# Applying the SSD's group norm to the tiles in the SSD stage instead of to the output projection's partial sums

## The chip, the cores and the metric

One core of a Trainium2 chip runs the whole layer. The metric is the device time of one execution in microseconds (us). An execution keeps five engines busy: TensorE (PE in the profile, with its weight loads as PEld), VectorE (DVE), ScalarE (ACT), GpSimd (POOL) and SyncE (SP), which issues nearly all DMAs here. Each engine works through its own instructions in a fixed order and waits where an operand is not ready.

## The reference, cut to what matters

The layer mixes two branches of 1024 columns each, a Mamba-2 SSD and a stick-breaking attention, projects their concatenation and goes on to a SwiGLU FFN. The part that the change concerns is the end of the SSD branch: two groups of 512 columns, each with its own RMS norm after the gate.

```python
y = y.reshape(bsz, seq, D_SSD) * silu(z)
yg = y.reshape(bsz, seq, SSD_GROUPS, D_SSD // SSD_GROUPS)
yg = yg * rsqrt(mean(yg * yg, axis=-1, keepdims=True) + EPS)
y_ssd = yg.reshape(bsz, seq, D_SSD) * norm_w
...
mix = concatenate([y_ssd, y_sb], axis=-1) @ w_out
```

The norm's factor is one number per token and group. It can be applied to the tile, or to the product of that group's 512 columns with `w_out`, which is linear in them.

## The kernel before, in words

Matrix products run as three fp32r products of high and low halves (`mm3`, line 55). The sequence is cut into 8 chunks of 128 tokens (`TB`), the SSD into 2 groups (`NG`) of 512 columns.

**SSD stage (lines 531 to 705).** `ssd_group(g)` (635) walks the 8 chunks in steps of two (`SC`, 650; a "part"). For each part it emits `ssd_front` of both chunks (550: transposes, the state's recurrence, the start of the tile `yy`), then `ssd_diag` of both (601: decay tiles `seg` on DVE and ACT, the products `pyd`, their addition to `yy`), then `ssd_gate` of both (618). The gate makes the product `pz` of 24 matmuls, its Silu `sz` on ACT, the multiplication of `yy` on DVE (626) and the Square on ACT with the sums of squares accumulated into a column of `yssq` (627). Then it turns the tile at once: four PE transposes into `pyt` (630), an ACT copy into `yt` (632, one buffer) and the store of `yt` to `yssd_s` through SP (633). The tile that is stored is not yet normed. Between group 0 and group 1 stand the blocks `x_block(1, b)`, 24 matmuls `px` for each half, with their convolution on POOL and DVE.

In this stage the order is not written out by hand for PE: the list `chain` (36 to 47), which fixes PE's order elsewhere, is off. A planner draws up each engine's order when the program is compiled; earlier instructions of the program have priority, and it works with costs of its own. So matmuls of `pz`, of `px` and, in group 1, of the attention's first projections `pp` stand between those of fronts and diags. Pools: `pss` has two PSUM banks under tag "a" (`pt`, `px_t`, `pyt`) and two under "b"; `psz` has two for `pz`; `yy` has four buffers.

**The norm's factor** is computed once after the SSD stage, for all 16 columns of `yssq`, by `rsqrt` on POOL (112, called in 1003): 2 instructions and three Newton steps of 4 on POOL (of 3 on DVE).

**Attention (714 to 1030).** Pairs of heads are worked off as "atoms" sorted by due times; PE's order is chained from due time -0.25 on. The atoms of the last pair's time hold the first 384 columns of the SSD half of the output projection as well: `a0_load` (938) fetches a block of `yssd_s`, `a0_split` (944) splits it on ACT and POOL, `a0_block` (950) multiplies. For each of the 8 token blocks it takes a bank `poa` of pool `psp` (two banks) for group 0 and another for group 1, 12 matmuls each. Group 0's bank is read by ACT with the factor as scale (962), group 1's by DVE, which scales and adds (964).

**Rest of the SSD half (1080 to 1096).** `out_a` does the other 640 columns in two parts of 320 (`ct`), again with one bank `po` (pool `psg`, four banks) for each group, 12 matmuls, an ACT read (1087) and a DVE read (1089) for each part. Beside it the weights of the attention half are loaded, multiplied by the gate row and split (`out_weights`, 1059), and `x_add` (1098) adds the residual on POOL. Then `b_norm` (1138) adds the attention half, and the FFN follows.

Of the kernel before, what the change touches and what calls it, by code (L numbers as in the profile page):

```python
# [7 lines left out]
F32 = mybir.dt.float32  # L8
F32R = mybir.dt.float32r
I32 = mybir.dt.int32  # L10
AF = mybir.ActivationFunctionType
ALU = mybir.AluOpType
# [3 lines left out]
P = 128  # L16
S = 1024
D = 1024
KT = D // P
TB = S // P  # L20
H = 16
HD = 64
NG = 2
# [6 lines left out]
def build(tc, t, dbg=None, stop=None):  # L30
    nc = tc.nc
# [23 lines left out]
    def mm3(out, sh, sl, mh, ml, start, stop, more=False):  # L55

        mm(out, sh, mh, start, False, more)
        mm(out, sh, ml, False, False, more)
        mm(out, sl, mh, False, stop, more)
# [47 lines left out]
    yssq = const.tile([P, NG * TB], F32, name="yssq")  # L107
# [4 lines left out]
    def rsqrt(n, src, scale, tag, eng=None):  # L112

        e = eng or nc.vector
        v = tiny.tile([P, max(n, 4)], F32, tag=tag + "v", name="rs_v")[:, 0:n]
        y = tiny.tile([P, max(n, 4)], F32, tag=tag + "y", name="rs_y")[:, 0:n]
        u = tiny.tile([P, max(n, 4)], F32, tag=tag + "u", name="rs_u")[:, 0:n]
        e.tensor_scalar(out=v, in0=src, scalar1=scale, scalar2=EPS, op0=ALU.mult, op1=ALU.add)  # L118
        e.tensor_scalar(out=y.bitcast(I32), in0=v.bitcast(I32), scalar1=-0.5, scalar2=RSQRT_MAGIC,
                        op0=ALU.mult, op1=ALU.add)  # L120
        for _ in range(3):
            e.tensor_tensor(out=u, in0=y, in1=y, op=ALU.mult)
            if eng is None:
                e.scalar_tensor_tensor(out=u, in0=u, scalar=-0.5, in1=v, op0=ALU.mult, op1=ALU.mult)
                e.scalar_tensor_tensor(out=y, in0=u, scalar=1.5, in1=y, op0=ALU.add, op1=ALU.mult)
            else:
                e.tensor_tensor(out=u, in0=u, in1=v, op=ALU.mult)
                e.tensor_scalar(out=u, in0=u, scalar1=-0.5, scalar2=1.5, op0=ALU.mult, op1=ALU.add)
                e.tensor_tensor(out=y, in0=u, in1=y, op=ALU.mult)  # L129
        return y  # L130
# [46 lines left out]
    def ps(name, tag=None):  # L177
        pcount[0] += 1
        return pss.tile([P, 512], F32, tag=tag or "ab"[pcount[0] & 1], name=name)
# [298 lines left out]
    def ada_step():  # L478

        on = chain["on"]  # L480
        for j in list(accs):
            acc = accs.pop(j)
            chain["on"] = True
            if j < 2:
                g1_row(j, acc)
            else:
                ada_cols(j, acc, ps("pc_"))
            if j == 5:
                nc.vector.scalar_tensor_tensor(out=sc2, in0=modT[:, 8:16], scalar=1.0, in1=n2T, op0=ALU.add, op1=ALU.mult)
        chain["on"] = on  # L490
        if ada_js:
            j = ada_js.pop(0)
            accs[j] = ada_acc(dtp, j, "adacc", 1, "adraw", 2)
# [107 lines left out]
    def ssd_diag(g, c, scT, xdt, yy):  # L601
        pyd = ps("pyd", "b")
        for q in range(2):
            seg = sq.tile([P, 4, P], F32, tag="seg", bufs=3, name="seg")
            r0 = (c * H + g * 8 + q * 4) * P
            dma(out=seg.rearrange("p h l -> p (h l)"), in_=csT_rows[:, r0:r0 + 4 * P].broadcast_to([P, 4 * P]))
            h0 = c * H + g * 8 + q * 4
            nc.vector.tensor_tensor(out=seg, in0=cs[:, h0:h0 + 4].unsqueeze(2).to_broadcast([P, 4, P]), in1=seg,
                                    op=ALU.subtract)
            nc.scalar.activation(seg, seg, AF.Relu)  # L610
            act_order("exp", nc.scalar.activation(seg, seg, AF.Exp, scale=-1.0))
            nc.vector.tensor_tensor(out=seg, in0=seg, in1=scT.unsqueeze(1).to_broadcast([P, 4, P]), op=ALU.mult)
            for i in range(4):
                hs = slice((q * 4 + i) * HD, (q * 4 + i + 1) * HD)
                mm(pyd[:, hs], seg[:, i], xdt[:, hs], True, True)
        nc.vector.tensor_tensor(out=yy, in0=yy, in1=pyd, op=ALU.add)

    def ssd_gate(g, c, zw, yy):

        tok = slice(c * P, (c + 1) * P)  # L620
        pz = psz.tile([P, 512], F32, tag="pz", name="pz")
        for k in range(KT):
            mm3(pz, hh[k][:, tok], hl[k][:, tok], zw[k][:, 0], zw[k][:, 1], k == 0, k == KT - 1)
        sz = sq.tile([P, 512], F32, tag="sz", bufs=2, name="sz")
        act_order("silu", nc.scalar.activation(sz, pz, AF.Silu))
        nc.vector.tensor_tensor(out=yy, in0=yy, in1=sz, op=ALU.mult)
        nc.scalar.activation(sz, yy, AF.Square, accum_out=yssq[:, g * TB + c:g * TB + c + 1])
        pyt = ps("pyt", "a")
        for i in range(4):
            nc.tensor.transpose(out=pyt[:, i * P:(i + 1) * P], in_=yy[:, i * P:(i + 1) * P], identity=ident)  # L630
        yt = sq.tile([P, 4, P], F32, tag="yt", bufs=1, name="yt")
        nc.scalar.copy(yt.rearrange("p a b -> p (a b)"), pyt)
        dma(out=yssd_s[c, :, 4 * g:4 * g + 4], in_=yt)

    def ssd_group(g):
        zw = load_z_weights(g)
        prev = None
        for c in range(0, TB, SC):
            part = []
            for cc in range(c, c + SC):  # L640
                part.append(ssd_front(g, cc, prev))
                prev = part[-1][3]
            for n, (scT, xdt, yy, _) in enumerate(part):
                ssd_diag(g, c + n, scT, xdt, yy)
            for n, (scT, xdt, yy, _) in enumerate(part):
                ssd_gate(g, c + n, zw, yy)
            if c in STEPS[g]:
                ada_step()

    SC = 2  # L650
    ssd_group(0)
# [8 lines left out]
    psp = aw.enter_context(tc.tile_pool(name="psp", bufs=2, side="right", space=PSUM))  # L660
    aw2 = ExitStack()
    apr = aw2.enter_context(tc.tile_pool(name="apr", bufs=1, side="right"))
    NP = H // 2
# [5 lines left out]
    CA = 3 * P  # L669
    w_pages, kp_t, qs_t, v_t = {}, {}, {}, {}  # L670
# [265 lines left out]
    y_pages, y_hl, x1_pages = [], {}, []  # L936
# [13 lines left out]
    def a0_block(i):  # L950
        hi, lo = y_hl[i]
        x1[i] = x1_pages[i]
        xo = x1[i][:, 0:CA]
        for g in range(NG):
            po = psp.tile([P, 512], F32, tag="pp", name="poa")[:, 0:CA]
            for k in range(4 * g, 4 * g + 4):
                w = w_pages[NP, k]
                mm3(po, hi[:, k], lo[:, k], w[:, 0], w[:, 1], k == 4 * g, k == 4 * g + 3)
                if k % 4 < 3:
                    yield  # L960
            if g == 0:
                nc.scalar.activation(xo, po, AF.Copy, scale=yr[:, i:i + 1])
            else:
                nc.vector.scalar_tensor_tensor(out=xo, in0=po, scalar=yr[:, TB + i:TB + i + 1], in1=xo,
                                               op0=ALU.mult, op1=ALU.add)
            yield

    def a0_atoms():
        t0 = NP - 1 + A0T
# [13 lines left out]
    NA = (D - CA) // 2  # L983
    wa, wa_pool = {}, []
# [15 lines left out]
            wa[ct, k] = hi, lo  # L1000
        return split

    yr = rsqrt(NG * TB, yssq, 1.0 / 512, "yn", nc.gpsimd)
    atoms = []
    for p in range(NP):
        atoms += attention_atoms(p, p == NP - 1)
# [26 lines left out]
    op1 = ou.enter_context(tc.tile_pool(name="op1", bufs=2, side="right", reuse_waits="tile"))  # L1033
# [33 lines left out]
    def out_mm(hi, lo, w, ct, n, ks=range(KT)):  # L1067
        po = (pso if n == 512 else psg).tile([P, 512], F32, tag="po" if n == 512 else "gu", name="po")[:, 0:n]
        for k in ks:
            mm3(po, hi[:, k], lo[:, k], *w[ct, k], k == ks[0], k == ks[-1])  # L1070
        return po
# [8 lines left out]
    def out_a(m, i):  # L1080

        for ct in range(2):
            xo = x1[i][:, CA + ct * NA:CA + ct * NA + NA]
            for g in range(NG):
                po = out_mm(*y_hl[i], wa, ct, NA, range(4 * g, 4 * g + 4))
                if g == 0:
                    nc.scalar.activation(xo, po, AF.Copy, scale=yr[:, i:i + 1])
                else:
                    nc.vector.scalar_tensor_tensor(out=xo, in0=po, scalar=yr[:, TB + i:TB + i + 1], in1=xo,
                                                   op0=ALU.mult, op1=ALU.add)  # L1090
        for n in (2 * m, 2 * m + 1):
            ct, k = n // KT, n % KT
            k = k ^ 4 if ct == 0 else k
            early = ct == 0 and k < 4
            w = opp.tile([P, S], F32R, tag="wb0" if early else "wb", bufs=4 if early else 12, name="wb")
            wb[ct, k] = out_weights(k, ct * 512, w[:, 0:512], w[:, 512:])
# [334 lines left out]
    po = None  # L1431
    for n, (ct, f) in enumerate(todo):
        if n + 2 < len(todo):
            loaded[n + 2] = down_load(*todo[n + 2])
        if f == 0:
            prev, po = po, []
        ah, al, w = made.pop(n)
# [39 lines left out]
```

## Time and profile before

| | |
|---|---|
| median of 3 runs | 1793.39 us (1791.37 to 1795.65) |
| profiled execution, its own time | 1794.46 us |
| its span in the trace | 1792.7 us |
| PE busy | 1719.0 us, 96% |
| DVE / ACT / POOL busy | 1193.9 / 814.4 / 358.6 us |
| mean granted TensorE clock | 0.992 |

The profile is that of one execution. Busy time is the time in which an engine works on an instruction; matmuls overlap, so a busy PE is one whose matmuls follow one another without a gap. "Idle before" is the time an engine stood still before a group of instructions, and the name behind the arrow is what ended that.

### The profile page before, as it was taken

The page shows a single profiled execution, that of the slowest core. Times are in us where ns is not written, and L with a number is a line of the kernel's source. Part 1 is how long each engine was busy: PE and PEld are TensorE (multiplying, and loading weights), DVE is VectorE, ACT ScalarE, POOL GpSimd, SP SyncE. Part 2 cuts the span into 40 slices and gives each one's busy share as a digit, 9 for nine tenths or more (in the row PEclk, how much of TensorE's full clock was granted, in tenths as well). Part 3 has the DMA queues.
Part 4 walks back from the last instruction along what each step waited for, and adds up shares of the span by engine and source line. Part 5 has one row for each costly group of instructions (what it writes and reads, how often), then busy time and mean ns, then how long its engine had stood idle before and what let it go on. Part 6 is the DMA issues. An engine that isn't in the chain of part 4 may idle for free.

```text
span 1792.7 us, 24476 instructions
## 1 busy us (share of the span) xinstructions
PE 1719.0 (96%) x9025; PEld 1400.9 (78%) x9025; DVE 1193.9 (67%) x1778; ACT 814.4 (45%) x1612; POOL 358.6 (20%) x652
## 2 busy tenths in 40 slices
PE   2999999999999999999899999899999999999999
PEld 2777777787787787787678888688888888788887
DVE  5497895756776776776876665976676666554541
ACT  4545562555565565565574345623333333422320
POOL 5420001033542542542621620000000000000000
PEclk9999999999999999999899999999999999999999
DMA  8366455311101101101223432542232222744721
GB/s 273 113 220 204 125 179 153 110 54 39 42 23 32 42 23 32 42 23 32 88 90 123 162 133 84 155 138 77 88 118 77 87 85 77 254 166 150 241 89 47
DMA packets 175790, 192.16 MB, mean 107 GB/s; under 512 B 11559, under 2 KB 126515, under 8 KB 175670
## 3 DMA queue, kind: packets, MB, share of 16 engines
q1 hardware_dynamic: 174582, 190.07, 33.5%
q8 instruction: 71, 1.16, 0.3%
q10 hardware_dynamic: 1088, 0.52, 0.1%
q14 instruction: 49, 0.40, 0.1%
HBM read 155.88 MB, written 34.67 MB: 106 GB/s over the span
## 4 chain that ended last, share of the span: by engine, by line
PE 66%; DVE 15%; POOL 6%; DMA 5%; issue 4%; ACT 3%; SPq 1%; DVEq 0%; POOLq 0%; ACTq 0%
PE pdn L50 13%; PE pX L50 10%; PE pp L50 7%; PE pY L50 6%; PE pZ L50 6%; DVE pr L838 5%; PE px L50 5%; PE po L50 4%; PE pz L50 3%; PE pa L50 2%; PE ptw L53 2%; PE pl L50 2%; DVE be L840 2%; PE pyd L50 2%; PE poa L50 1%
## 5 line engine op out<-in xcount | busy, mean ns | idle before, releaser
L50 PE MATMUL pp<-wp,hh 128*128 128x384 f32 x1024 | 288.0, 361 | 8.2 <-DVE wp L688 8.1
L50 PE MATMUL pdn<-dw,ah 128*128 128x512 f32 x704 | 217.0, 389 | 1.8 <-DVE t L1312 1.8
L50 PEld LDWEIGHTS pp<-wp,hh 128*128 128x128 f32 x1024 | 172.1, 189 | 51.1 <-issue 39.2
L838 DVE TENSOR_TENSOR_SCAN pr<-pr,idz 128x256 f32<-128x256 f32 (+7 forms) x128 | 174.0, 1389 | 1.5 <-ACT pr L833 1.5
L50 PE MATMUL pp<-wp,hl 128*128 128x384 f32 x512 | 173.0, 338 | 0.0
L50 PEld LDWEIGHTS pdn<-dw,ah 128*128 128x128 f32 x704 | 132.0, 188 | 29.8 <-DVE t L1312 2.3
L50 PE MATMUL pdn<-dw,al 128*128 128x512 f32 x352 | 136.9, 389 | 0.0
L855 ACT COPY wt<-ptw 128x512 f32<-128x512 f32 (+1 forms) x160 | 88.5, 559 | 76.4 <-PE ptw L53 76.3
L833 ACT ACTIVATE pr<-pl 128x384 f32<-128x384 f32 (+3 forms) x192 | 95.8, 499 | 52.8 <-PE pl L50 45.8
L1412 ACT CAST ah<-araw 128x1024 fp32r<-128x1024 f32 x44 | 46.4, 1055 | 144.4 <-PE pdn L50 130.3
L1276 ACT CAST wl<-s 128x512 fp32r<-128x512 f32 x88 | 54.9, 623 | 123.6 <-PE pX L50 42.6
L65 DVE TENSOR_TENSOR wl<-s,wl 128x512 fp32r<-128x512 f32 x88 | 60.6, 692 | 67.7 <-ACT wl L1276 66.9
L840 DVE TENSOR_TENSOR be<-be,pr 128x256 f32<-128x256 f32 (+7 forms) x128 | 99.6, 807 | 3.9
L53 PE MATMUL ptw<-ident,be 128*128 128x128 f32 x576 | 91.1, 276 | 6.2 <-DVE be L840 6.2
L50 PEld LDWEIGHTS pp<-wp,hl 128*128 128x128 f32 x512 | 96.5, 188 | 0.2 <-issue 0.2
L834 ACT ACTIVATE be<-pl 128x384 f32<-128x384 f32 (+3 forms) x192 | 96.4, 502 | 0.0
L784 DVE TENSOR_TENSOR qkraw<-qkraw,rs_y 128x256 f32<-128x256 f32 x64 | 31.2, 527 | 95.6 <-POOL rs_y L129 95.6
L65 DVE TENSOR_TENSOR al<-araw,ah 128x1024 fp32r<-128x1024 f32 x44 | 53.7, 1223 | 58.4 <-ACT ah L1412 57.5
L50 PE MATMUL pz<-zw,hh 128*128 128x512 f32 x256 | 90.5, 422 | 0.0
L118 POOL TENSOR_SCALAR rs_v<-qkred 128x8 f32<-128x8 f32 x32 | 25.2, 787 | 305.7 <-DVE qkred L779 305.7
L53 PEld LDWEIGHTS ptw<-ident,be 128*128 128x128 f32 x576 | 72.0, 141 | 14.7 <-DVE be L840 5.6
L1276 ACT CAST wl<-raw 128x512 fp32r<-128x512 f32 x62 | 38.5, 622 | 98.2 <-PE pY L50 41.0
(373 smaller groups left out, 4162.1 us busy)
## 6 DMA issues: line engine op xcount, KB each, us to landing
araw<-a_s SPq DMA_DIRECT2D x44, 512.0 KB, 3.4
adaraw<-in_w_ada_dram SPq DMA_DIRECT2D x64, 256.0 KB, 3.3
wraw<-in_w_in_dram SPq DMA_DIRECT2D x64, 192.0 KB, 3.1
raw<-in_w_gate_dram SPq DMA_DIRECT2D x46, 256.0 KB, 3.0
raw<-in_w_up_dram SPq DMA_DIRECT2D x44, 256.0 KB, 3.2
draw<-in_w_down_dram SPq DMA_DIRECT2D x44, 256.0 KB, 3.4
ada_raw<-in_w_ada_dram SPq DMA_DIRECT2D x16, 512.0 KB, 5.6
seg<-csT_s SPq DMA_DIRECT2D x32, 256.0 KB, 3.2
```

The lines of the kernel that those rows point to most:

```text
L50: link(nc.tensor.matmul(out, lhsT, rhs, start=start, stop=stop, skip_group_check=more))
L53: link(nc.tensor.transpose(out=out, in_=in_, identity=identity or ident))
L65: return nc.vector.tensor_tensor(out=lo, in0=src, in1=f32(hi), op=ALU.subtract)
L118: e.tensor_scalar(out=v, in0=src, scalar1=scale, scalar2=EPS, op0=ALU.mult, op1=ALU.add)
L784: inst = nc.vector.tensor_tensor(out=r4[:, t2], in0=r4[:, t2], in1=r[:, t2].unsqueeze(2).to_broadcast([P, 4, HD]), op=ALU.mult)
L833: nc.scalar.activation(pr[:, c0:c1], pl[:, 0:c1 - c0], AF.Sigmoid, scale=-1.0)
L834: nc.scalar.activation(be[:, c0:c1], pl[:, 0:c1 - c0], AF.Sigmoid)
L838: nc.vector.tensor_tensor_scan(out=rev, data0=rev, data1=idz[:, S - n:][:, ::-1], initial=0.0, op0=ALU.mult, op1=ALU.max)
L840: nc.vector.tensor_tensor(out=be[:, 0:n], in0=be[:, 0:n], in1=pr[:, 1:n + 1], op=ALU.mult)
L855: nc.scalar.copy(wt[:, 0:m], pt[:, 0:m])
L1276: nc.scalar.copy(w[:, 0], src)
L1412: nc.scalar.copy(ah, raw)
```

## The change

The gate leaves the tile unturned. A new function `ssd_norm` scales it on ACT by the norm's factor and then turns, copies and stores it. `norms()` works off the parts that wait: it computes the factor of a part's two columns by `rsqrt` on DVE and calls `ssd_norm` for both chunks. It is called in each step between the diags and the gates, for the part before, and once more behind each group. In the projection the two groups of a block share one bank: 24 matmuls, then one plain ACT copy. The factor on POOL and the DVE reads are gone.

```diff
@@ ssd_gate
         nc.scalar.activation(sz, yy, AF.Square, accum_out=yssq[:, g * TB + c:g * TB + c + 1])
+
+    def ssd_norm(g, c, yy, r):
+        nc.scalar.activation(yy, yy, AF.Copy, scale=r)
         pyt = ps("pyt", "a")
         for i in range(4):
             nc.tensor.transpose(out=pyt[:, i * P:(i + 1) * P], in_=yy[:, i * P:(i + 1) * P], identity=ident)
         yt = sq.tile([P, 4, P], F32, tag="yt", bufs=1, name="yt")
         nc.scalar.copy(yt.rearrange("p a b -> p (a b)"), pyt)
         dma(out=yssd_s[c, :, 4 * g:4 * g + 4], in_=yt)
+
+    unnormed = []
+
+    def norms():
+
+        for g, c, yys in unnormed:
+            r = rsqrt(SC, yssq[:, g * TB + c:g * TB + c + SC], 1.0 / 512, "yn")
+            for n, yy in enumerate(yys):
+                ssd_norm(g, c + n, yy, r[:, n:n + 1])
+        unnormed.clear()
@@ ssd_group
                 ssd_diag(g, c + n, scT, xdt, yy)
+            norms()
             for n, (scT, xdt, yy, _) in enumerate(part):
                 ssd_gate(g, c + n, zw, yy)
+            unnormed.append((g, c, [x[2] for x in part]))
             if c in STEPS[g]:
                 ada_step()
+        norms()
@@ a0_block
-        for g in range(NG):
-            po = psp.tile([P, 512], F32, tag="pp", name="poa")[:, 0:CA]
-            for k in range(4 * g, 4 * g + 4):
-                w = w_pages[NP, k]
-                mm3(po, hi[:, k], lo[:, k], w[:, 0], w[:, 1], k == 4 * g, k == 4 * g + 3)
-                if k % 4 < 3:
-                    yield
-            if g == 0:
-                nc.scalar.activation(xo, po, AF.Copy, scale=yr[:, i:i + 1])
-            else:
-                nc.vector.scalar_tensor_tensor(out=xo, in0=po, scalar=yr[:, TB + i:TB + i + 1], in1=xo,
-                                               op0=ALU.mult, op1=ALU.add)
-            yield
+        po = psp.tile([P, 512], F32, tag="pp", name="poa")[:, 0:CA]
+        for k in range(KT):
+            w = w_pages[NP, k]
+            mm3(po, hi[:, k], lo[:, k], w[:, 0], w[:, 1], k == 0, k == KT - 1)
+            if k < KT - 1:
+                yield
+        nc.scalar.copy(xo, po)
+        yield
@@
-    yr = rsqrt(NG * TB, yssq, 1.0 / 512, "yn", nc.gpsimd)
@@ out_a
-            for g in range(NG):
-                po = out_mm(*y_hl[i], wa, ct, NA, range(4 * g, 4 * g + 4))
-                if g == 0:
-                    nc.scalar.activation(xo, po, AF.Copy, scale=yr[:, i:i + 1])
-                else:
-                    nc.vector.scalar_tensor_tensor(out=xo, in0=po, scalar=yr[:, TB + i:TB + i + 1], in1=xo,
-                                                   op0=ALU.mult, op1=ALU.add)
+            nc.scalar.copy(xo, out_mm(*y_hl[i], wa, ct, NA))
```

## Rows read from the trace of the kernel before

**Rows 1.** The page: busy time by engine, and the chain by engine.
```profile
PE 1719.0 (96%) x9025; PEld 1400.9 (78%) x9025; DVE 1193.9 (67%) x1778; ACT 814.4 (45%) x1612; POOL 358.6 (20%) x652
...
PE 66%; DVE 15%; POOL 6%; DMA 5%; issue 4%; ACT 3%; SPq 1%; DVEq 0%; POOLq 0%; ACTq 0%
```

**Rows 2.** Busy time by stretch; its first line names the columns.
```profile
core 0: us, PE busy (x) PEld busy (x) DVE busy (x) ACT busy (x) POOL busy (x), PEclk, DMA share, GB/s
150.00:285.00 135.00, 134.19 (x671) 105.87 (x670) 110.89 (x168) 76.39 (x124) 6.83 (x9) 1.00 0.51 160
...
303.00:392.00 89.00, 87.44 (x487) 71.44 (x486) 66.13 (x111) 44.65 (x84) 9.09 (x28) 1.00 0.34 105
392.00:405.00 13.00, 13.00 (x79) 12.96 (x78) 4.54 (x9) 3.99 (x11) 10.33 (x42) 1.00 0.06 22
...
870.00:960.00 90.00, 80.07 (x506) 61.20 (x503) 68.12 (x68) 53.82 (x113) 28.02 (x23) 0.94 0.24 78
960.00:1022.00 62.00, 59.23 (x391) 57.39 (x390) 46.84 (x58) 25.75 (x42) 30.21 (x19) 1.00 0.53 172
```

**Rows 3.** PE's waits, 140 to 400: total us, times, longest.
```profile
PE pt L556 <- DMA xc<-xbc_s: 1.8, 1, 1.8
PE pyo L50 <- DVE state L588: 0.7, 1, 0.7
PE pyt L630 <- DVE yy L626: 0.6, 1, 0.6
```

**Rows 4.** PE's groups, 870 to 1022: busy, mean ns, idle before.
```profile
L50 PE MATMUL poa<-wp,y_page 128*128 128x384 f32 x192 | 44.7, 367 | 5.0 <-DVE x L964 2.6 <-POOL y_page L947 2.2
L50 PE MATMUL po<-wa,yhi 128*128 128x320 f32 x144 | 36.5, 312 | 1.8 <-DVE x L1089 1.8
L50 PE MATMUL po<-wa,ylo 128*128 128x320 f32 x96 | 29.9, 311 | 0.9 <-DVE ylo L65 0.9
L53 PE MATMUL ptw<-ident,be 128*128 128x128 f32 x102 | 17.3, 287 | 5.0 <-DVE be L840 5.0
```

**Rows 5.** `poa`'s matmuls, the banks' four reads: ns min/median/max, first and last start.
```profile
L50 PE MATMUL poa<-wp,y_page x192: 331/338/689, 871.9 to 954.5; 128*128 128x384 f32 x192
...
L962 ACT ACTIVATE x<-poa,rs_y x8: 582/596/662, 883.1 to 948.8; 128x384 f32<-128x384 f32 x8
L964 DVE SCALAR_TENSOR_TENSOR x<-poa,rs_y,x x8: 590/608/618, 894.6 to 955.0; 128x384 f32<-128x384 f32 x8
...
L1087 ACT ACTIVATE x<-po,rs_y x16: 519/523/529, 961.2 to 1018.2; 128x320 f32<-128x320 f32 x16
...
L1089 DVE SCALAR_TENSOR_TENSOR x<-po,rs_y,x x16: 536/544/551, 963.0 to 1020.1; 128x320 f32<-128x320 f32 x16
```

**Rows 6.** DVE in order of time: the last Newton step of a later rsqrt.
```profile
1072.15 0.15 DVE L122 TENSOR_TENSOR rs_u<-rs_y 128x1 f32<-128x1 f32 x1
1072.34 0.16 DVE L124 SCALAR_TENSOR_TENSOR rs_u<-rs_u,rs_v 128x1 f32<-128x1 f32 x1
1072.53 0.16 DVE L125 SCALAR_TENSOR_TENSOR rs_y<-rs_u,rs_y 128x1 f32<-128x1 f32 x1
```

**Rows 7.** ACT scaling a 128x512 tile by a column, in a later stage.
```profile
L1152 ACT ACTIVATE hn<-x,rs_y x8: 724/728/729, 1041.9 to 1120.5; 128x512 f32<-128x512 f32 x8
```

**Rows 8.** PE and ACT in order of time: turns of two parts, the stage's end.
```profile
340.57 0.60 PE L630 MATMUL pyt<-ident,yy 128*128 128x128 f32 x4
...
346.16 0.60 PE L630 MATMUL pyt<-ident,yy 128*128 128x128 f32 x4
...
405.63 0.55 PE L50 MATMUL pl<-kp,qv 64*128 64x128 f32 x6
...
390.73 0.19 ACT L627 ACTIVATION_READ_ACCUMULATOR sz<-yy 128x1 f32 x1
```

**Rows 9.** The store of `yt`, at the foot of that tile's view.
```profile
DMA to landing us min/median/max: 2.0/2.3/3.0
```

**Rows 10.** POOL in order of time: the norm factor's first instruction.
```profile
393.15 0.45 POOL L118 TENSOR_SCALAR rs_v<-yssq 128x16 f32<-128x16 f32 x1
```

## The prediction, written before the changed kernel was run

> **What bounds the kernel now.** I read the page first: PE is busy for 96% of the span and makes up 66% of the chain that ended last, DVE comes second in both [rows 1]. So a part of the change is worth what it takes from PE's gaps or adds to them; work moved between the other engines is worth nothing unless a gap of PE hangs on it. The view of busy time by stretch then says where gaps lie [rows 2]: in the SSD stage PE works 134.2 of 135 us before group 1 and 87.4 of 89 in it, in the stretch with the first 384 columns of the projection only 80.1 of 90, in the one with the other 640 columns 59.2 of 62. The view of PE's waits names what ends them. In the SSD stage the three longest are a load (1.8 us), the state (0.7) and a turned tile that waits for its gate (0.6, once in 16 turns) [rows 3]. In the projection 2.6 us of the gap before `poa` and 1.8 before `po` end with the DVE read of the bank that PE wants again; 2.2 us end with a split on POOL, 0.9 with one on DVE, and 5.0 before the attention's turns with the product `be` on DVE [rows 4].
>
> **What is removed.** Per block of tokens the change takes away one of two reads of `poa` and two of four reads of `po`: 8 DVE instructions of 0.608 us and 16 of 0.544, together 13.6 us of DVE [rows 5]. The 8 and 16 ACT reads stay, as plain copies in place of scaled ones (0.596 and 0.523 us); I count no difference. A bank is now claimed for 24 matmuls, not 12. The 16 half blocks of `poa` run from 871.9 to 954.5, so pool `psp` (two banks) hands one out each 5.2 us and the reader has about that long; with 8 whole blocks it has 10.3 us for a 0.6 us copy [rows 5]. `po` has four banks and half as many claims. So the waits on lines 964 and 1089, 2.6 + 1.8 = 4.4 us of PE, should go whole, and PE, which is the path at that point, gains them: **-4.4 us**. Bounds: 0 if the next wait takes it all, -4.4 for these two. What is late next is the split of the `y` blocks on DVE (0.9 us) and `be` (5.0 us) [rows 4]. The latter waits for scans that no removed read stands directly behind in the trace, so I count nothing for it.
>
> The `rsqrt` on POOL, 14 instructions of 0.2 to 0.45 us from 393.15 on [rows 10], had its consumer at 883 [rows 5]. Behind it on POOL stand some memsets and the norm of the attention's second unit. POOL is 10.3 of 13 us busy there, but PE has no gap [rows 2]: **0**. If that cover were gone it would be worth its own 4.4 us at most.
>
> **What is added.** (a) Eight `rsqrt` on DVE for two columns each: 2 + 3 x 3 = 11 instructions, 88 in all. The same step on one column starts its instructions 0.19 us apart [rows 6], so a chain takes 2.1 us and the eight 16.7 us. That is more than the 13.6 us that DVE is spared, but in the SSD stage, where DVE is 111 of 135 and 66 of 89 us busy [rows 2]; with some 8 us more in each it stays at 88% and 84%. On PE's path: 0 as long as PE has other matmuls ready.
>
> In the rows a 0.15 us instruction on one column stands beside 0.6 us for one on 384 columns [rows 5, 6]. [...]
>
> (b) Sixteen scalings on ACT. Nearest row: the same form on 128x512, 0.728 us [rows 7], 11.6 us in a stage where ACT is busy 121 of 224 us [rows 2]. On the path 0, with the same cover.
>
> (c) Turns, copies and 16 stores stay as many but come a part later. The copy has one buffer, whose store takes 2.3 us to land [rows 9]. Now a part's two turns stand 5.6 us apart [rows 8], so the second copy never meets the first's store; behind one `rsqrt` both come together, and the second may stand in ACT's queue for about 2.3 us, with the Relu and Exp of the next decay tiles behind it. On SP the stores move past the loads of `xc` and `seg` for the next part; where a store waits for `yt`, those loads wait behind it. The bound is 8 x 2.3 = 18 us of ACT's queue; I take 0 of PE, because 24 matmuls of `pz` for each chunk and the blocks `px` and `pp` can be put in between.
>
> (d) PE's order is fixed in advance. A turn now has a chain of 2.1 + 0.7 = 2.8 us ahead of it instead of nothing but the product on DVE. If the planner places it too early, PE stands. Above, 2.8 us at each of eight parts, 22.6 us; below, -0.6 us, the wait that the old turns had [rows 3]. Of these I take **+0.6**, one more wait of that kind, being nearest to the row of the same turns.
>
> (e) The end of group 1. The last sums of squares are read at 390.9 [rows 8]. Behind them now come the 2.1 us chain, two scalings and the last turns, about 4 us. PE is full from 392 to 405 with projections `pp`, and the first logits `pl`, which want the banks of pool `pss`, come at 405.6 [rows 2, 8]. **0**; without the `pp` it would be 4 us.
>
> **The sum.** 1794.46 - 4.4 + 0.6 = 1790.7 us for the profiled execution (span 1792.7 plus 1.8 around it). That execution lay 1.07 us above the median, so I predict **1789.6 us**, 3.8 below the median. A measurement of this kernel can tell about 0.2%, 3.6 us, from no change; the forecast stands at that edge.
>
> **Rivals.** *More is gained.* DVE is spared in the stretches where its `be` and its splits hold PE up for 5.0 and 0.9 us [rows 4]. If half of the first and all of the second go too, 3.4 us more: 1786. For it: DVE works 68 of 90 and 47 of 62 us there [rows 2]. Against: the removed reads are 4.9 and 8.7 us of that and mostly not ahead of a late scan.
>
> *The gain is given back.* PE is freed from one wait and meets the next (the `y` split on DVE, the weights' DMA behind it), or one or two parts of the SSD stage lose 2.3 us each to the single `yt`: 2 to 4 us, 1792 to 1794. For it: two of the four rows name other work of DVE [rows 4]. Against: PE in the SSD stage has hardly a gap [rows 3].
>
> *Slower: the turns stall PE in the SSD stage.* The chain of 11 short instructions is late against the planner's costs, and PE, in its fixed order, waits in front of the turn in each of eight parts. It decides from 4.4 / 8 = 0.55 us per part; at half of the 2.8 us it costs 11.3 us: 1794.46 - 4.4 + 11.3 - 1.07 = 1800. For it: rsqrt chains cannot be shortened by free engines, and the trace of before shows none of this length ahead of a PE instruction in this stage. Against: a turn waited once in 16 times, for 0.6 us [rows 3], and DVE chains there are placed well. That the planner does not keep the turns one step behind, but puts them right behind the factor, is part of this case.
>
> **Chances.** Forecast 0.45, its two sides of the 0.2% bound 0.26 and 0.19; more gained 0.18; given back 0.21; slower 0.16. So faster 0.26 + 0.18 = 0.44, same 0.19 + 0.21 = 0.40, slower 0.16. The range runs from 1785, the larger gain with 1 us to spare, to 1797.5, which is the stall at 1 us per part (8 us on 1790.1 less 1.07 gives 1797.0); left out are about half of the slow case and a little below.
>
> **What would show it.** No wait of PE on DVE's reads of `poa` and `po`, because there are none, and no new one on ACT's copies; the stretch of the projection about 4 us shorter. DVE in the SSD stage some 15 us busier with PE's gaps as before, about 4 us in all. The last turns near 395 with PE full to 405. It is wrong if PE's waits from 150 to 392 name the scaled `yy` or the copy `yt` for more than 2 us, or if the 4.4 us turn up in front of `ptw`, `poa` or `po` under other names.

## The result, and the profile after

The changed kernel takes 1806.3 us (median of 4 runs, 1804.14 to 1809.74) against 1794.0 us for the kernel before on the same chip: ratio 1.0066, 95% interval 1.0052 to 1.0080. It is slower by some 12 us; 1789.6 was forecast, with a range up to 1797.5. The profiled execution took 1807.11 us with a span of 1805.4, 12.7 us longer than the span before.

The page first, in the two lines that answer to [rows 1]:

```profile
PE 1724.9 (96%) x9025; PEld 1406.9 (78%) x9025; DVE 1190.9 (66%) x1842; ACT 823.7 (46%) x1630; POOL 353.5 (20%) x638
...
PE 68%; DVE 15%; POOL 5%; DMA 5%; issue 3%; ACT 3%; SPq 0%; DVEq 0%; POOLq 0%; ACTq 0%
```

They hardly differ from before: an average over the whole span hides a stall of 12 us. The stretches of the SSD stage, as in [rows 2], show it:

```profile
core 0: us, PE busy (x) PEld busy (x) DVE busy (x) ACT busy (x) POOL busy (x), PEclk, DMA share, GB/s
150.00:285.00 135.00, 132.62 (x663) 104.33 (x662) 112.38 (x211) 80.69 (x130) 8.70 (x9) 1.00 0.50 156
303.00:392.00 89.00, 80.63 (x401) 63.44 (x400) 68.62 (x138) 45.92 (x79) 7.10 (x17) 0.92 0.37 111
392.00:405.00 13.00, 12.87 (x77) 12.16 (x77) 5.23 (x22) 5.84 (x13) 1.23 (x7) 0.92 0.06 23
```

In group 1 of the SSD stage (303 to 392) PE now works 80.6 us of 89, at a mean granted clock of 0.92; before it was 87.4 at 1.00. The milestones on PE agree. The last `px` matmul before group 1 moves from 284.5 to 289.4 (+4.9), the last turn `pyt` from 390.7 to 404.5 (+13.8), the first logits `pl` from 405.6 to 420.6 (+15.0). From there the changed kernel wins back 2.2: from the first `pl` to the first `pX` of the FFN 734.2 us in place of 735.4, from there to the last `pdn` 646.4 in place of 647.4. So the whole loss lies in the SSD stage. From 150 us to the first `pl` PE stands still for 10.9 us (259.72 busy of 270.60); before it was 4.2 (251.41 of 255.60).

PE's waits from 140 to 420, to be held against [rows 3]:

```profile
PE px_t L564 <- DVE scT L561: 2.9, 1, 2.9
PE pt L556 <- DMA xc<-xbc_s: 1.8, 3, 1.4
PE pt L556 <- issue: 1.4, 1, 1.4
PE px_t L564 <- DVE yy L568: 1.4, 1, 1.4
PE pyt L633 <- ACT yy L630: 1.0, 1, 1.0
PE pyt L633 <- DVE scT L561: 0.8, 1, 0.8
```

The turns wait 1.0 us for the scaled `yy`, hardly more than the old turns for their gate. The new waits stand at the *front* of a part (`pt`, `px_t`), on work that has nothing to do with the norm. The worst place is the last part of group 1. PE, in order of time, with the wait ahead of an instruction in brackets:

```profile
368.27 0.34 PE L50 MATMUL pp<-wp,hl 128*128 128x384 f32 x1
369.60 0.33 PE L633 MATMUL pyt<-ident,yy 128*128 128x128 f32 x1 [0.99 <-ACT yy L630]
370.53 1.10 PE L50 MATMUL pyd<-xdt,seg 128*128 128x64 f32 x8 [0.61 <-DVE seg L612]
371.48 0.93 PE L633 MATMUL pyt<-ident,yy 128*128 128x128 f32 x7
372.65 0.33 PE L556 MATMUL pt<-ident,xc 128*128 128x128 f32 x1 [0.24 <-ACT yt L635]
372.81 0.39 PE L50 MATMUL pt<-xc 128*128 128x128 f32 x2
376.05 0.66 PE L564 MATMUL px_t<-ident,xc 128*128 128x128 f32 x4 [2.85 <-DVE scT L561]
378.13 0.45 PE L556 MATMUL pt<-ident,xc 128*128 128x128 f32 x1 [1.43 <-issue]
...
387.28 0.99 PE L50 MATMUL pp<-wp,hh 128*128 128x384 f32 x2
```

Read from the top. The first turn waits 0.99 us for the scaled tile. This wait is not what makes the next instructions late: the `pyd` matmuls behind it wait another 0.61 us for their own `seg`. DVE finished that one at 370.48, since it stood in DVE's order behind the subtraction of another `seg`, whose load DVE awaited for 1.42 us (the first two lines below). The `pyd` matmuls free a decay buffer, SP issues the next `seg` load at 371.67, and DVE waits for that one too, with `scT` next in its queue:

```profile
369.19 0.69 DVE L608 TENSOR_TENSOR seg<-cs,seg 128x512 f32<-128x512 f32 x1 [1.42 <-DMA seg<-csT_s]
369.80 0.68 DVE L612 TENSOR_TENSOR seg<-seg,scT 128x512 f32<-128x512 f32 x1
...
375.10 0.69 DVE L608 TENSOR_TENSOR seg<-cs,seg 128x512 f32<-128x512 f32 x1 [2.02 <-DMA seg<-csT_s]
375.71 0.28 DVE L561 TENSOR_TENSOR scT<-pt,tri 128x128 f32<-128x128 f32 x1
...
377.35 0.68 DVE L568 TENSOR_TENSOR yy<-px_t,bc 128x512 f32<-128x512 f32 x1
```

Meanwhile the two turns have held both banks of tag a. The first `pt` waits for the copy `yt` (0.24 us). `px_t` waits 2.85 us for `scT`, which is DVE's read of that `pt` bank: the other bank still holds the second turn, whose copy begins at 376.33, behind other work of ACT. The second `pt` begins at 378.13, when DVE's read of the `px_t` bank has ended (377.35 + 0.68); there the profile says "issue", since it shows no releaser. No `pz` and no `pp` stands in PE's order to fill the gaps, from 368.6, where the last `pp` ends, to 387.28. In the kernel before, `pp` matmuls stand between the same turns and fronts (between `pt` and `px_t`, 371.95 to 372.91, for one).

ACT, in order of time, in the same part:

```profile
367.00 1.28 ACT L611 ACT_TABLE_LOAD   x1
...
368.83 1.32 ACT L630 ACTIVATE yy<-yy,rs_y 128x512 f32<-128x512 f32 x2
...
376.33 0.58 ACT L635 COPY yt<-pyt 128x512 f32<-128x512 f32 x1
```

In stretches of 10 us, of the changed kernel (columns as above):

```profile
360.00:370.00 10.00, 8.94 (x52) 7.38 (x50) 7.13 (x21) 8.66 (x12) 0.00 (x0) 1.00 0.22 79
370.00:380.00 10.00, 4.95 (x29) 4.09 (x30) 6.62 (x13) 7.53 (x15) 0.00 (x0) 0.85 0.23 80
380.00:390.00 10.00, 9.43 (x32) 7.06 (x30) 6.46 (x13) 2.71 (x7) 0.92 (x2) 0.50 0.08 26
390.00:400.00 10.00, 10.00 (x55) 9.83 (x55) 3.88 (x14) 4.03 (x11) 2.74 (x13) 0.80 0.00 0
```

of the same kernel, the stretch at the lower clock by itself:

```profile
376.90:394.00 17.10, 15.30 (x51) 12.74 (x52) 10.33 (x22) 5.72 (x13) 3.66 (x14) 0.50 0.09 31
```

and of the kernel before, where the same part runs:

```profile
370.00:380.00 10.00, 8.97 (x52) 7.24 (x51) 8.40 (x16) 7.28 (x15) 4.44 (x14) 1.00 0.14 52
380.00:390.00 10.00, 10.00 (x72) 9.96 (x71) 6.95 (x12) 3.53 (x8) 1.01 (x4) 1.00 0.17 54
```

PE works 4.95 us of 10, and then a second loss follows that the kernel before does not have in this stage: the granted clock is 0.50 from 376.9 to 394.0, where its rows have 1.00. PE looks busy from 380 to 390 (9.43 us) and gets through 32 instructions, where the kernel before has 72. Three `pp` matmuls that take 0.52 us at the full clock (from 394.48 to 395.00) took 0.96 here (391.05 to 392.01). By these rows the 15.3 us that PE worked at the lower clock would have been about 8 at the higher one. So this tail is some 7 us, an estimate, of the 15.0 at the first `pl`; the 6.7 us more in which PE stands still are most of the rest.

Why is the scaled tile late? For the turn at 369.60 the chain ends at 366.68, 6.3 us after it began, and then ACT has a Silu, a table load of 1.28 us and an Exp ahead of the scaling (368.83). The chain's own part of that is seen best on DVE, in order of time, on the chain of another part (its 11 instructions are those on 128x2):

```profile
212.11 0.16 DVE L118 TENSOR_SCALAR rs_v<-yssq 128x2 f32<-128x2 f32 x1
212.18 0.69 DVE L587 TENSOR_TENSOR state<-state,ex 128x512 f32<-128x512 f32 x1
213.18 0.69 DVE L616 TENSOR_TENSOR yy<-yy,pyd 128x512 f32<-128x512 f32 x1 [0.31 <-PE pyd L50]
213.79 0.16 DVE L119 TENSOR_SCALAR rs_y<-rs_v 128x2 int32<-128x2 int32 x1
214.53 0.69 DVE L608 TENSOR_TENSOR seg<-cs,seg 128x512 f32<-128x512 f32 x1 [0.58 <-DMA seg<-csT_s]
215.14 0.15 DVE L122 TENSOR_TENSOR rs_u<-rs_y 128x2 f32<-128x2 f32 x1
```

and the two ends of the longest chain:

```profile
375.91 0.16 DVE L118 TENSOR_SCALAR rs_v<-yssq 128x2 f32<-128x2 f32 x1
...
397.86 0.15 DVE L125 SCALAR_TENSOR_TENSOR rs_y<-rs_u,rs_y 128x2 f32<-128x2 f32 x1
```

DVE's order puts one instruction of the chain between other tiles' work, again and again. The eight chains take 3.7, 12.8, 5.2, 9.6, 4.0, 6.3, 22.1 and 2.1 us from first to last instruction; only the last, with nothing beside it, takes the 2.1 that I had assumed for all. But the longest, 22.1 us, costs PE no wait: `pp` matmuls stand in its order until those turns come (398.85), and PE is busy without a gap from 386 to 400.

The projection's rows, PE's groups from 870 to 1035, answer to [rows 4]:

```profile
L50 PE MATMUL poa<-wp,y_page 128*128 128x384 f32 x192 | 43.9, 365 | 2.2 <-POOL y_page L963 2.2
L50 PE MATMUL po<-wa,yhi 128*128 128x320 f32 x144 | 37.1, 317 | 0.0
L50 PE MATMUL po<-wa,ylo 128*128 128x320 f32 x96 | 30.6, 319 | 4.1 <-DVE ylo L65 4.0
L53 PE MATMUL ptw<-ident,be 128*128 128x128 f32 x119 | 20.2, 286 | 7.0 <-DVE be L856 6.9
```

The 4.4 us of waits on DVE's reads are gone, as forecast. In their place `ylo` has grown from 0.9 to 4.0 and `be` from 5.0 to 6.9, together 5.0 more.

### The profile page after: what moved, and what is told of

The parts are those of the page before. It is cut to its first block, busy times and chain, and to the rows that moved or that the text cites. A ratio compares the mean times of both kernels' runs of the same rounds, so it can differ in the third digit from the quotient of the medians.

```text
span 1805.4 us, 24519 instructions
## 1 busy us (share of the span) xinstructions
PE 1724.9 (96%) x9025; PEld 1406.9 (78%) x9025; DVE 1190.9 (66%) x1842; ACT 823.7 (46%) x1630; POOL 353.5 (20%) x638
## 4 chain that ended last, share of the span: by engine, by line
PE 68%; DVE 15%; POOL 5%; DMA 5%; issue 3%; ACT 3%; SPq 0%; DVEq 0%; POOLq 0%; ACTq 0%
PE pdn L50 13%; PE pX L50 10%; PE pp L50 7%; PE pY L50 6%; PE pZ L50 6%; PE po L50 6%; DVE pr L854 5%; PE px L50 5%; PE pz L50 3%; PE pa L50 2%; PE ptw L53 2%; DVE be L856 2%; PE pyd L50 2%; PE pl L50 1%; PE poa L50 1%
## 5 line engine op out<-in xcount | busy, mean ns | idle before, releaser
L50 PE MATMUL pz<-zw,hh 128*128 128x512 f32 x256 | 84.2, 406 | 0.0
```

The source lines that it names most:

```text
L50: link(nc.tensor.matmul(out, lhsT, rhs, start=start, stop=stop, skip_group_check=more))
```

## The experiments

Two theories stood against each other. **Late factor**: each turn hangs on a factor whose chain comes late in DVE's order, and what stands behind the turn is late with it. **Crowded turns**: the turns of a part, both together and one part later, fight for the banks of tag a and the single `yt`, with or without a factor. A third, that the 88 small instructions merely take up DVE, was tried too. Every ratio is to the kernel before on the same chip. The last two columns come from each kernel's profile: the first `pl` (end of the SSD stage) and the time from the first `poa` to the first `pX` (the projection and what follows it).

| kernel | ratio (95% interval) | first `pl`, us | `poa` to `pX`, us |
|---|---|---|---|
| before | 1 | 405.6 | 269.1 |
| changed | 1.0066 (1.0052 to 1.0080) | 420.6 | 269.2 |
| proj_only | 0.9992 (0.9978 to 1.0006) | 409.0 | 265.8 |
| norm_only | 1.0106 (1.0091 to 1.0121) | 424.5 | 270.0 |
| late_only | 0.9988 (0.9973 to 1.0003) | 409.2 | 266.4 |
| no_chain | 0.9997 (0.9981 to 1.0012) | 407.6 | 266.1 |
| chain_unused | 0.9988 (0.9973 to 1.0004) | 405.5 | 266.7 |
| pool_chain | 1.0215 (1.0190 to 1.0241) | 450.0 | 266.0 |
| yt_in_yy | 1.0027 (1.0010 to 1.0044) | 417.2 | 267.2 |
| two_steps | 1.0059 (1.0035 to 1.0083) | 415.4 | 266.6 |
| chain_early | 0.9985 (0.9973 to 0.9998) | 409.5 | 267.6 |
| early_yy | 1.0002 (0.9986 to 1.0018) | 411.8 | 268.3 |
| late2 | 1.0000 (0.9986 to 1.0015) | 409.6 | 266.6 |
| apart | 1.0072 (1.0051 to 1.0093) | 423.9 | 267.2 |
| act_store | 1.0038 (1.0021 to 1.0056) | 417.4 | 267.4 |
| early_act | 1.0005 (0.9988 to 1.0021) | 411.2 | 266.7 |
| early_norm_only | 0.9999 (0.9983 to 1.0016) | 409.7 | 272.3 |

One caution on reading it: each edit makes the planner lay out the whole stage afresh. The SSD stage of proj_only is written as before, and yet its first `pl` comes 3.4 us later. So 3 or 4 us in the `pl` column are no effect of what an edit was meant to do. The same holds of the last `px` before group 1: late_only, as fast as before, has it at 288.3. The last two columns show one execution each: that of two_steps was the fastest of five (1800.5, median 1805.9), that of early_norm_only the slowest of ten (1803.5, median 1796.2).

The six slowest kernels stood longest at the lower clock. From 150 us to the first `pl` the granted clock was 0.50 for 17.1 us in the changed kernel and in norm_only, 20.5 in apart, 10.2 in two_steps and act_store, 6.8 in yt_in_yy, chain_early and early_act, 3.4 in no_chain and early_yy, 37.5 in pool_chain, and never in before, proj_only, late_only, chain_unused, late2 and early_norm_only.

### The two halves

proj_only is the kernel before with the diff's hunks on `poa` and `out_a` alone. norm_only is the changed kernel with the two-bank projection put back:

```
 for g in range(NG):
     po = out_mm(*y_hl[i], wa, ct, NA, range(4 * g, 4 * g + 4))
     if g == 0:
         nc.scalar.copy(xo, po)
     else:
         nc.vector.tensor_tensor(out=xo, in0=po, in1=xo, op=ALU.add)
```

> The projection's part alone: the SSD stage as before (turns straight behind each gate, no factor), poa and po summed over all eight k in one bank and copied once; the group norm's factor is left out of the computation. If the whole loss sits in the SSD stage (my reading of the two traces), this is faster than before: the stretch from the first to the last poa matmul shrinks by 1.6 us or more and the time is 1789 to 1793 against 1794. If the projection's part itself costs (out_a lost 2.2 us in the trace after), it is 1794 to 1797.

> The SSD stage's part alone: factor, scaling and turns one part late as in the changed kernel, but the projection in two banks per part as before, the first half read by a plain ACT copy, the second added by DVE. If the loss sits in the SSD stage: 1806 to 1810, last turn near 404 as in the changed kernel. If the two parts only hurt together: under 1800.

The loss is the norm's: 1.0106 for it alone, no loss for the projection alone (0.9992). By the ratios norm_only is 7 us slower than the changed kernel; 3.9 of them stand at the first `pl` already (424.5), ahead of the projection, and the rest is not in its profile, which was its fastest run. In the last part of group 1 its PE order is that of the changed kernel, with the same waits and the same 17.1 us at a clock of 0.50.

### What of the norm

```
late_only:     r = yssq[:, g * TB + c:g * TB + c + SC]   # and no scaling in ssd_norm
no_chain:      ssd_norm(g, c + n, yy, ones[:, 0:1])      # no rsqrt
chain_unused:  r = rsqrt(SC, ...); ssd_norm(g, c + n, yy, ones[:, 0:1])
```

> The changed kernel without rsqrt chain and without scaling (the factor is left out of the computation): only the turns are one part late, both of a part together. If the lateness and pairing of the turns (two banks of tag a, single yt, in front of the next part's pt and px_t) is the cause: still slow, 1800 to 1806, and pt or px_t wait late in group 1. If the 2.1 us chain and the 0.7 us scaling ahead of the turn are the cause: 1788 to 1793, no late last turn (near 390 to 394).

> The changed kernel with the scaling by a constant column of ones and no rsqrt chain (the factor is left out of the computation). Pairing of turns: 1802 to 1807. If DVE's chain of 11 instructions is the cause: back to 1790 to 1794. If the ACT scaling is the cause: as slow as the changed kernel, while the kernel with late turns alone is fast.

> The changed kernel with the chain computed on DVE as it is, but the scaling by a constant column of ones, so that nothing waits for the chain (the factor is left out of what is computed). If the cost is how long the chain takes until its factor is there (4 to 22 us in the trace after, where it stands between other work of DVE, against 2.1 us assumed): fast, 1791 to 1796, ratio 1.000. If the cost is the place that 88 instructions take in DVE's queue: slow, 1802 to 1807.

All three are as fast as before. late_only refutes crowded turns as a cause by themselves: turns, copies and stores stand where the change has them. no_chain adds the 16 scalings, which cost nothing that can be measured. chain_unused has the 88 chain instructions on DVE and the 16 scalings. Its factors are there as late as in the changed kernel (worked out from the timelines, 12.2 us after the part's last Square in the mean of the eight parts and 24.2 in the worst, against 12.5 and 24.3); only nothing waits for them, and the 12 us are gone. So neither DVE's load nor the chain's length is the cause by itself; that the turns hang on the chain is.

By which way is not settled by this. When the turns hang on nothing, the planner lays another order as well: in chain_unused `pz` and `pp` matmuls stand again between the turns and fronts of the last parts. No run keeps the changed kernel's order and takes the dependence alone away. So whether PE loses by waiting for a late factor, or by the order that the planner lays for one, stays open for the changed kernel; its waits, 1.0 us for the scaled tile and far more for loads and banks, speak for the order.

### Another place for the chain

```
-            r = rsqrt(SC, yssq[:, g * TB + c:g * TB + c + SC], 1.0 / 512, "yn")
+            r = rsqrt(SC, yssq[:, g * TB + c:g * TB + c + SC], 1.0 / 512, "yn", nc.gpsimd)
```

> The changed kernel with the chain on POOL (14 instructions of about 0.2 us, 3 to 4 us where nothing stands between). If the chain's long way through DVE's shared queue is the cost: 1791 to 1797. If any wait of the turns for a factor costs, on whatever engine: 1800 or more.

That missed by far: 1.0215. PE's waits in it, from 140 to 440:

```profile
PE pyt L633 <- ACT yy L630: 26.0, 8, 6.5
PE pt L556 <- DMA xc<-xbc_s: 2.1, 1, 2.1
```

This is the slower rival of the prediction in pure form: eight waits of the turn for its factor, 26.0 us, with stretches at a clock of 0.50 behind them (37.5 us in all). POOL's chains take 4.1 to 8.3 us, and the factor is there 6.1 us after the part's last Square in the mean of the eight parts, sooner than in the changed kernel (12.5, both worked out from the timelines). Still it costs more: in this plan PE's order has the turns so early that all eight parts wait. So the time from sums to factor does not decide by itself; where PE's fixed order has the turn when the factor comes decides too.

The opposite move: the chain is written straight behind its own part's gates, and the turns stay where they were.

```
     def norms():
-        for g, c, yys in unnormed:
-            r = rsqrt(SC, yssq[:, g * TB + c:g * TB + c + SC], 1.0 / 512, "yn")
+        for g, c, yys, r in unnormed:
...
-            unnormed.append((g, c, [x[2] for x in part]))
+            r = rsqrt(SC, yssq[:, g * TB + c:g * TB + c + SC], 1.0 / 512, "yn")
+            unnormed.append((g, c, [x[2] for x in part], r))
```

> The changed kernel with the chain written straight behind the gates of its own part, before the fronts and decay tiles of the next, and the scalings and turns where the change has them. If the cost is that the factor comes late (the chain stands last in DVE's order of the part): 1792 to 1797, ratio 0.998 to 1.002, and no wait of PE on the scaled yy or on scT in front of px_t. If it is the pairing of the turns and the single yt: 1800 to 1806.

The whole loss goes: 0.9985. Nothing is left out, the instructions are those of the changed kernel but for two table loads fewer on ACT (35, not 37; late_only has 37 and is fast), and only their order differs. On DVE the chain is still spread between other work (6.7 to 9.5 us, the last 3.8), but it starts earlier: the factor is there 7.6 us after the part's last Square, in the mean of eight parts, and in no part later than 10.6, against 24.3 in the worst part of the changed kernel. PE's waits from 140 to 420 name neither the scaled `yy` nor `scT`:

```profile
PE pt L556 <- DMA xc<-xbc_s: 2.3, 2, 2.0
PE pyd L50 <- issue: 1.6, 1, 1.6
PE pq L53 <- DVE qkraw L800: 1.3, 1, 1.3
PE pyd L50 <- DVE seg L612: 1.0, 2, 0.8
```

It has the lowest ratio of the kernels that leave nothing out, though the intervals of the others with an early chain overlap it; against the kernel before its gain stays inside the 0.2%. In its last parts, too, `pp` matmuls stand between turns and fronts on PE. So what is shown is that the place of the chain in the program makes the loss; it acts on DVE's time and on the planner's order at once.

### The chain's length

two_steps has two Newton steps, 8 instructions a chain.

> The changed kernel with two Newton steps in place of three in the group norm's chain: 8 instructions, not 11. If the time follows the chain's length: a quarter of the loss comes back, 1802 to 1804. If it hangs on single collisions in a fixed order: anywhere between 1794 and 1806, by one or two waits that come or go in the last two parts of group 1.

1.0059: an interval that holds both the old loss and the quarter less, so it settles nothing by itself. The long chain near the end still takes 17.2 us (22.1 before): its length on the clock comes from what stands between its instructions.

### By which way the late turn costs

yt_in_yy copies the turned tile back into its own `yy` (`nc.scalar.copy(yy, pyt)`, five `yy` buffers, no `yt`). act_store issues the store with `nc.scalar.dma_start`, off SP's queue. apart calls the two turns of a part one by one, each ahead of its own gate.

> The changed kernel with each turned tile copied back into its own yy (five buffers in place of four), so that no copy waits for the store of the one before. If the single yt is the cost (copies that waited 2.4 and 2.0 us for a store, and the bank held until then): 8 us or more come back, 1796 to 1799. If the late factor is the cost: 1803 to 1806, with the copies' waits for stores gone.

> The changed kernel with the 16 stores of the turned tiles issued from ACT's DMA queue in place of SP's, so that a store that waits for its copy holds no load of seg or xc behind it; chain, turns and the single yt stay. If the loss comes through SP's order (the store stands on SP until the late copy, the seg load behind it, DVE behind that, then scT and px_t): at least 5 us come back, 1794 to 1801, and the wait of px_t on scT (2.9 us) goes. If the banks and the late turns alone make it: 1803 to 1807.

> The changed kernel with a part's two turns apart, each ahead of its own gate of the next part; the chain as in the changed kernel. If the pairing of the turns costs (both banks of tag a at once, the second copy behind the first's store): 1795 to 1800. If the late factor is the cost: 1802 to 1807.

yt_in_yy takes away 7 of the 12 us (1.0027), act_store about 5 (1.0038, an interval that just meets the changed kernel's); apart takes nothing (1.0072), and its `px_t` waits the same 2.9 us for `scT` (0.7 in act_store). The first two fell between the ranges that their expectations set. In yt_in_yy PE works 8.02 us from 370 to 380, not 4.95. So the loss shrinks without the single `yt` and with the stores off SP's queue. That `yt` itself holds PE up is not shown by this: in yt_in_yy the planner has put `pp` matmuls between the last turns and fronts as well, and in the changed kernel no copy waits for a store in the part where PE loses most. How the loss is divided between SP's order, the banks and the order of PE stays open: SP waited no longer for the copies than before in total (30.5 us against 33.4 from 150 to 410), and moving the stores changed the plan as well. The clock can be counted: 6.8 us at 0.50 in yt_in_yy and 10.2 in act_store, where the changed kernel has 17.1.

With the early chain the same edits have nothing left to take. early_yy and early_act are the early chain with yt_in_yy's and act_store's edit; late2 is early_yy with the turns put behind the next part's gates:

> Both: the chain straight behind its gates, and the turned tile copied back into its yy (five buffers). If late factor and single yt each cost by themselves: below either alone, 1790 to 1794, ratio under 1.000. If one of them is the whole cost: the same as the better of the two.

> The chain straight behind its gates, and the stores on ACT's queue. If the early chain has taken the whole loss away: as with the early chain alone, ratio 0.997 to 1.000. If SP's order still costs something there: under 0.997.

> As the kernel before this one, but the turns of a part stand behind the gates of the next part, not ahead of them: more time for the factor, turns later still. If only the lateness of the factor costs: 1790 to 1795. If late turns cost by themselves, at the end of group 1 above all, where two parts' turns then come together: 1796 to 1802.

1.0002, 1.0005 and 1.0000: no better than the early chain alone. late2 shows that turns still later, behind the next part's gates, do no harm when the factor is early. With early_norm_only below, all five kernels with the early chain run as before (0.9985 to 1.0005), and all six with the whole or shortened chain on DVE just ahead of the turns are slower (1.0027 to 1.0106). Most of them have layouts of their own, so one lucky layout is no explanation.

### The projection priced again

> The chain straight behind its gates, but the projection in two banks per part with two reads as before. Against the same kernel with one bank per part (ratio 0.9985) this prices the projection's part in a kernel whose SSD stage is not disturbed. If its 4.4 us of waits on the reads are a gain of their own: 1.0005 to 1.0015, 4 us slower than with one bank. If they are given back to the next waits (ylo and be): 0.998 to 1.000, no difference.

0.9999 against 0.9985 for one bank. The intervals overlap, so the two ratios alone settle neither 0 nor 4.4 us. The last column of the table says more, one execution for each kernel: the three kernels with two banks take 269.1, 270.0 and 272.3 us from `poa` to `pX`, the fourteen with one bank 265.8 to 269.2, median 266.7. That is 2.4 us under the kernel before, and the changed kernel's own profile is the slowest of the fourteen. (The 272.3 is early_norm_only's, in its slowest run.) proj_only's waits from 865 to 1035 show where the rest went:

```profile
PE poa L50 <- POOL y_page L947: 4.3, 1, 4.3
PE ptw L53 <- DVE be L840: 4.0, 3, 1.9
PE po L50 <- DVE ylo L65: 3.1, 2, 1.8
```

No wait on a read is left, `be` is 1.0 shorter, but the splits on POOL and DVE hold PE up for 4.3 and 3.1 us in place of 2.2 and 0.9.

## Why the prediction was wrong

**The step that failed is (a) with (d).** (a) gave each chain 2.1 us and PE "0 as long as PE has other matmuls ready"; (d) priced a turn's lateness by the wait of the turn itself and took +0.6. The wait of the turn was indeed 1.0 us. Two things were wrong. The dependent chains in DVE's full, fixed queue did not take the sum of their instructions, 2.1 us: seven of the eight took 3.7 to 22.1 us. And the cover that (a), (b) and (c) rest on, matmuls of `pz`, `px` and `pp` that "can be put in between", was not there: from 368.6 to 387.28 PE's order has none of them, and PE stands at the next part's `pt` and `px_t`. What stands in place of +0.6 is 15.0 us at the first `pl`: 6.7 us more in which PE stands still, and some 7 (the estimate above) from 17.1 us at half clock, a term that the prediction does not have. That the loss comes from where the chain is written is shown (chain_unused, chain_early). Whether the late factor makes it at run time or through the order that the planner lays for it stays open.

The other terms, in the prediction's order.

*The waits on the reads, -4.4.* The waits went whole. Of the gain some 2.4 us stay in the median of the one-bank kernels and none in the changed kernel's own execution, where `ylo` and `be` took 5.0. The rival "given back" named the right successor for this half.

*The factor on POOL, 0, and (b), the scalings, 0.* Nothing speaks against either: no_chain has the scalings and no POOL factor, and runs as before. A scaling took 0.712 us in the median, 0.728 was assumed.

*DVE's load in (a).* Right: the 88 chain instructions, forecast at 16.7 us, cost nothing where nobody waits (chain_unused, 0.9988). A single one took 0.15 to 0.17 us in 87 of 88 cases, the duration in [rows 6].

*(c), the single `yt`, 0 of 18.* Right with an early chain (early_yy gains nothing). With the late one copies do wait, that at 406.72 for 1.96 us for the store before it, and 7 us come back without `yt`; how much of them is `yt` and how much the new plan is open.

*(e), the end of group 1, 0.* The shape held: in the changed kernel the last chain begins at 400.0 and the last matmul of the last turn at 404.5, and PE is full from 392 to 405, though at a clock of 0.92. From there to the first `pl` it takes 16.1 us, before 14.9. What came late was the last gate itself: its sums were read at 400.0, before at 390.9.

*The slower rival* had the right sign and the right engine, and its 1800 for a wait in each of eight parts was nearer than the forecast. Its mechanism, PE standing in front of the turn, is what pool_chain shows; in the changed kernel PE stands one step further on, and the half clock was in neither. Its 0.16 was too little: that the trace of before shows no chain of this length ahead of PE in this stage was a reason to give it more.

## What to carry to other kernels

Price a small dependent chain by the queue that it stands in, not by the sum of its instructions; where the order is fixed ahead of time, write it straight behind its inputs, so that it is done long before the step that needs it. When a step becomes later and a planner fixes the order, look at what it puts behind the step: cover that "can be put in between" counts only where the order has it, and read the granted clock behind a stall of PE as well as the stall: here it was 0.50 for 17.1 us behind one of some 5. And a wait that is removed is worth what the next one leaves of it.

## What the runs showed of the hardware that was not expected

The half clock. After PE had worked 4.95 us from 370 to 380, with no single wait over 2.85 us, the granted clock was 0.50 from 376.9 to 394.0, and a `pp<-wp,hl` matmul took 0.52 us in place of 0.34, though PE was busy for 15.3 of those 17.1 us. So behind a stall of some 5 us stood a tail of some 7 us (the estimate above) that no wait names.

On POOL the chain's instructions take 0.2 us each in the median, as in the factor that was removed, but from the third on they start 0.27 to 0.29 us apart even where nothing comes between, and a chain of 14 lasts 4.1 to 8.3 us; DVE's 11 start 0.19 to 0.21 us apart and last 2.1.
